# All later conditioning in layer 0 in rows of 1024 columns, three attention scalings on ScalarE, output rows transposed later

## The chip, the cores and the metric

The kernel runs on one core of a Trainium2 chip. The metric is the device time of one execution in microseconds. TensorE (PE) multiplies matrices, with its weight loads shown apart as PEld. VectorE (DVE), ScalarE (ACT) and GpSimd (POOL) work on elements, and SyncE (SP) issues most of the transfers.

## The reference

A two-layer diffusion trunk in fp32 over 640 tokens: 128 of context and 512 latent, 2048 features each. Cut to what matters here:

```
m = silu(cond) @ ada_w[layer] + ada_b[layer]        # one row for context (c_ctx), one for latent (c)
sh, sc, gt = split(m, 3)                            # 3 x 2048 columns
h = rms_norm(x, g) * (1 + sc) + sh
# layer 0: mixer A (windowed attention with a sink logit per head, rotary) and mixer B (gated short convolution)
# layer 1: mixer C (differential attention: o1 - lam * o2, then an RMS norm) and mixer D (dense attention)
p = softmax(q @ k.T * scale)                        # with the sink as one more logit in mixer A
out = concat(branches, each times silu(gate)) @ w_out
x = x + gt * out
```

The input projections have 2048 rows and some fifty tiles of 128 columns in each layer. The results are x of both groups and the new keys and values.

## The kernel before

**Products.** An fp32 operand is split into a rounded high part and a low part. A product is three matmuls into one sum: high weights by high data, high weights by low data, low weights by high data. Tokens stand in columns, in two halves of 320 (`pa`, `pb`).

**Input projection.** `run_tiles` goes over jobs, one for each tile of 128 output columns; layer 0 has 52. A job has four quarters of four 128-row weight blocks. For each quarter `load_raw` fetches 256 KB (SyncE's queue), `split_w` makes `wh` on ScalarE (L232) and `wl` on VectorE (L233), and `proj_q` issues 24 matmuls (L267 to L269), which last some 3.5 us. In layer 0 the first jobs are worked on side by side, and six of them are held as sums in a pool "lead" on the right side of the memory.

**Fill.** Behind each quarter stands a `slot`. It moves the generators on by a step: those that prepare keys, queries and values (`k_gen`, where `kg` is the gained key, multiplied by the rotary tables into `m` at L586 to L590, and transposed on TensorE at L545), the attention that is under way, and a "fill" with a rate, so many steps for each slot.

**Conditioning.** The fill is `ada_on_dve`. It forms blocks of 512 columns of silu(cond) @ ada_w on VectorE: for each of 16 row blocks it loads a tile `adaw` and does a multiply-add into `acc` for each of the two conditions (L202 for the first row block, L204 for the others). Four matmuls with `ones` then add over partitions (L210), ScalarE copies the result, two transposes turn it, and the bias is added. Twelve blocks lie in layer 0 (rate 1.2, a step for each row block). Four lie in layer 1, in halves of 256 columns (rate 0.9, from job 25 on).

**Attention.** `scores` issues the score matmuls `S` (L706 to L710). `soft` takes the negated maximum `nm` on VectorE (L673), scales it (L677 with a sink in layer 0, L675 without in layer 1), takes the exponential on ScalarE (L680, with the row sum `l`), and the reciprocal `rl` (L686). The probabilities `p` are scaled by `rl` in the pair attention (L766, VectorE) and transposed on TensorE (L694) into `T`. Differential attention scales its output by `rls` (L1323, VectorE).

**Output projection.** `project_out` does four tiles of 128 output features singly, and the others in a 2 x 2 form that saves products: `forms` combines halves of the mixed features, and sums of weight blocks (`sx`, `sf`, from L453 on) are multiplied by `run_pairs` (L516 to L518). For a finished tile, `res_load` fetches the old x as `xr`, `res_sum` adds the gated product (L1074), and `finish` in layer 1 transposes the tile with five matmuls `T<-ident,xr` (L545 in `rows_out`), since the results have tokens in rows.

**Order.** The generators set the order in which the program is written, and the language's scheduler moves instructions from there. So the order on an engine is neither the written one nor independent of what else is written.

Of the kernel before, what the change touches and what calls it, by code (L numbers as in the profile page):

```python
# [20 lines left out]
P = 128  # L21
# [24 lines left out]
SPLIT_AHEAD = 3  # L46
N_FILL0 = 12
FILL0 = 1.2
FILL1 = 0.9
FILL1_FROM = 24  # L50


@with_exitstack
def trunk_kernel(ctx: ExitStack, tc: tile.TileContext, I: dict, O: dict):
# [12 lines left out]
    def psT():  # L67
        return pT.tile([P, 512], F32, tag="T", name="T")
# [112 lines left out]

    def ada_on_dve(blocks, tags, parts=1, tie=lambda: None):


        wt, wd = tags[2:5], 512 // parts
        bufs = 3 if wt[0] == wt[1] else 1
        for l, cb in blocks:
            ap = pools["cur"]
            acc = [ap.tile([P, 512], F32, tag=tags[c], name=f"acc{c}", bufs=1) for c in range(2)]
            mark = tie()  # L190
            if mark is not None:
                for c in range(2):
                    V.tensor_copy(acc[c][:, 0:1], mark)
            for i in range(KT * parts):
                kt, h = i % KT, i // KT
                w = ap.tile([P, wd], F32, tag=wt[i % 3], name="adaw", bufs=bufs)
                c0 = cb * 512 + h * wd
                nc.sync.dma_start(w, I["ada_w"][l, kt * P:(kt + 1) * P, c0:c0 + wd])
                for c in range(2):
                    a = acc[c][:, h * wd:(h + 1) * wd]  # L200
                    if kt == 0:
                        V.tensor_scalar(a, w, sT[:, kt, c:c + 1], None, ALU.mult)  # L202
                    else:
                        V.scalar_tensor_tensor(out=a, in0=w, scalar=sT[:, kt, c:c + 1], in1=a,  # L204
                                               op0=ALU.mult, op1=ALU.add)
                yield
            s = psT()
            for g in range(4):
                c, h = g // 2, g % 2
                PE.matmul(s[32 * g:32 * g + 32, 0:256], ones, acc[c][:, h * 256:(h + 1) * 256],  # L210
                          start=True, stop=True, tile_position=(0, 32 * g))
            sb = ap.tile([P, 256], F32, tag=tags[5], name="ada_sb2", bufs=3 if tags[5] == wt[0] else 1)
            A.copy(sb, s[:, 0:256])
            t = psT()
            for j in range(2):
                PE.transpose(t[:, j * P:(j + 1) * P], sb[:, j * P:(j + 1) * P], ident)
            t = t[:, 0:256].rearrange("p (j c h x) -> p h j c x", j=2, c=2, h=2)
            for h in range(2):
                add_bias(l, cb, t[:, h, :, :, 0], h, 2)
            ada_done(l, cb)  # L220
            ready.add((l, cb))
            yield

    ready = set()

    def need(l, n, fill):
        while (l, 8 + n // 4) not in ready:
            next(fill)

# [70 lines left out]
    def run_tiles(jobs, w_ap, make_h, fill=None, rate=0.0, ahead=None, order=(0, 1, 2, 3), before=None,  # L300
                  last=None, by_half=False, trans=[], grace=0, cut=None, summed=None, led=None, fill_from=0, lead_in=None):
        if trans:
# [13 lines left out]
        for ui, (pos, qd, js) in enumerate(units):  # L316
            raws = {n: load_raw(w_ap, jobs[n][0], qd, js) for n in leads[:W_BUFS]}
            if ui == 0 and lead_in:
                lead_in()
            parts = {n: split_w(raws[n]) for n in raws}  # L320
# [350 lines left out]
    def soft(ap, width, s, n, rsc, nsink=None, sink=None):  # L671
        nm = small.tile([P, 1], F32, tag="nm", name="nm")
        V.tensor_reduce(nm, s, axis=AX.X, op=ALU.max, negate=True)  # L673
        if sink is None:
            V.tensor_scalar(nm, nm, rsc, None, ALU.mult)  # L675
        else:
            V.tensor_scalar(nm, nm, rsc, nsink, ALU.mult, ALU.min)  # L677
# [55 lines left out]
    def pair_gen(ap, width, k, banded, emit, done, sinks):  # L733
# [27 lines left out]
        def score(u, j):  # L761
# [3 lines left out]
            p, rl, _ = soft(ap, width, s[:, lo:hi], hi - lo, q[2][u], *sinks[j])  # L765
            V.tensor_scalar(p[:, 0:hi - lo], p[:, 0:hi - lo], rl, None, ALU.mult)  # L766
            ps.setdefault(u, []).append(p)

        for u in range(6):
# [12 lines left out]
            if u < 5:  # L782
# [19 lines left out]

    ada_rest = [(0, cb) for cb in range(8, 12)] + [(1, cb) for cb in (4, 0, 5, 1, 6, 2, 7, 3, 8, 9, 10, 11)]
# [97 lines left out]
    def even_start():  # L901
        close("start")
        open_pool("even")


# [108 lines left out]
    for i in range(4, 8):  # L1014
# [4 lines left out]
    run_tiles(jobs, I["ev_w_in"][0], h0_maker, fill0, FILL0, ada_group, trans=TRANS, grace=GRACE, cut=((0, 2), (2, 4)),  # L1019
              summed=keep, led=even_start)  # L1020
    drain(prep)
    for _ in fill0:
        pass

    N_SINGLE = (4, 4)
# [63 lines left out]
    def project_out(l, maker, finish, last, tail):  # L1089
# [45 lines left out]
        def later(n):  # L1135
            yield
            finish(n)
# [146 lines left out]
    def diff_gen(ap, h, gt):  # L1284
# [28 lines left out]
        def weigh(u):  # L1313
# [62 lines left out]
    for n in range(4):  # L1376
# [14 lines left out]
    def y1_maker(k):  # L1391
        if k == 4:
            for _ in fill1:
                pass
            drain(attn)
# [91 lines left out]
```

## Time and profile before

| | |
|---|---|
| runs, us | 2334.67, 2336.52, 2340.44 (median 2336.52) |
| the profiled execution | 2336.23 us; its span 2334.4 us, 1.8 us lie outside it |
| PE (weight loads) busy | 2286.5 us, 98% (2209.1 us, 95%) |
| DVE busy | 1591.4 us, 68% |
| ACT busy | 950.3 us, 41% |
| POOL busy | 134.4 us, 6% |
| transfers | 321.98 MB, 138 GB/s over the span |

Rows of the profile name the engine, the line, the operation with out<-in, the number of instructions, the busy time and the mean of one in ns, and then the idle time of the engine ahead of them with what ended it. Rows of the timeline have start and length in us, and in brackets the idle time ahead. Rows of the stretches (windows) have the time from start to end in us, the length, the busy time of each engine with its number of instructions, the granted clock of TensorE (1.00 is full), the share of the DMA engines and GB/s.

### The profile page before, as it was taken

How to read it: one execution, taken by the hardware profiler on the slowest of the kernel's cores; microseconds unless marked ns; L12 is line 12 of the kernel's file. 1: busy time of each engine (PE TensorE's matmuls, PEld its weight loads, DVE VectorE, ACT ScalarE, POOL GpSimd, SP SyncE). 2: the span in 40 equal slices, each digit the busy share in tenths (PEclk: the TensorE clock that was granted, in tenths of full speed). 3: DMA queues.
4: the chain of work that ended last, by engine and by line, in shares of the span. 5: the costliest groups of instructions: out<-in, count | busy, mean ns of one | idle time of the engine just before them, and what ended most of it. 6: DMA issues, size and time to landing. Idle time of an engine off the chain costs nothing.

```text
span 2334.4 us, 41910 instructions
## 1 busy us (share of the span) xinstructions
PE 2286.5 (98%) x16092; PEld 2209.1 (95%) x16092; DVE 1591.4 (68%) x3246; ACT 950.3 (41%) x2006; POOL 134.4 (6%) x183
## 2 busy tenths in 40 slices
PE   7999999999999999999999999999999999999999
PEld 5889999999999999899999999999999999999999
DVE  4668887777777774877855755755756754568665
ACT  5335532433422223544554434344334444445443
POOL 1001000000000000000010100101000001000001
PEclk9999999999999999999999999999999999999999
DMA  9986345435355554844431422413323312128542
GB/s 324 292 263 200 105 121 171 142 113 168 118 180 168 169 158 135 263 136 134 150 97 52 144 70 78 141 51 106 112 73 96 102 46 82 49 73 283 156 136 60
DMA packets 399208, 321.98 MB, mean 138 GB/s; under 512 B 18834, under 2 KB 353136, under 8 KB 398496
## 3 DMA queue, kind: packets, MB, share of 16 engines
q1 hardware_dynamic: 391008, 288.94, 41.6%
q0 software_dynamic: 7280, 28.20, 3.2%
q8 instruction: 126, 2.06, 0.4%
q10 hardware_dynamic: 720, 2.16, 0.3%
q14 instruction: 74, 0.61, 0.1%
HBM read 290.79 MB, written 28.44 MB: 137 GB/s over the span
## 4 chain that ended last, share of the span: by engine, by line
PE 48%; DVE 4%; DMA 3%; ACT 1%; issue 1%; POOL 0%; SPq 0%; DVEq 0%; POOLq 0%; ACTq 0%
PE pa L267 4%; PE pb L268 4%; PE pb L267 4%; PE pb L269 4%; PE pa L269 4%; PE pa L268 4%; PE pq L518 4%; PE pq L517 4%; PE pq L516 4%; PE T L694 1%; DMA adaw<-in_ada_w 1%; PE S L706 1%; PE S L708 1%; PE S L707 1%; DMA yin<-yd 1%
## 5 line engine op out<-in xcount | busy, mean ns | idle before, releaser
L232 ACT ACTIVATE wh<-raw 128x512 fp32r<-128x512 f32 (+1 forms) x504 | 303.9, 604 | 782.7 <-PE pb L268 651.8
L267 PE MATMUL pa<-h,wh 128*128 128x320 f32 x1728 | 551.5, 319 | 3.5 <-ACT h L232 3.0
L268 PE MATMUL pa<-h,wh 128*128 128x320 f32 x1728 | 537.4, 311 | 2.8 <-DVE h L233 2.8
L233 DVE TENSOR_TENSOR wl<-raw,wh 128x512 fp32r<-128x512 f32 (+1 forms) x504 | 330.2, 656 | 303.4 <-ACT wh L232 284.0
L269 PE MATMUL pa<-h,wl 128*128 128x320 f32 x1728 | 535.5, 310 | 0.0
L269 PE MATMUL pb<-h,wl 128*128 128x320 f32 x1728 | 535.0, 310 | 0.0
L268 PE MATMUL pb<-h,wh 128*128 128x320 f32 x1728 | 534.9, 310 | 0.0
L267 PE MATMUL pb<-h,wh 128*128 128x320 f32 x1728 | 534.6, 310 | 0.0
L204 DVE SCALAR_TENSOR_TENSOR acc<-adaw,sT,acc 128x512 f32<-128x512 f32 (+1 forms) x600 | 357.4, 641 | 23.0 <-DMA adaw<-in_ada_w 21.8
L267 PEld LDWEIGHTS pa<-h,wh 128*128 128x128 f32 x1728 | 325.4, 188 | 24.6 <-issue 16.6
L268 PEld LDWEIGHTS pa<-h,wh 128*128 128x128 f32 x1728 | 326.1, 189 | 6.3 <-DVE h L233 4.2
L269 PEld LDWEIGHTS pa<-h,wl 128*128 128x128 f32 x1728 | 325.6, 188 | 1.2 <-issue 1.2
L268 PEld LDWEIGHTS pb<-h,wh 128*128 128x128 f32 x1728 | 324.4, 188 | 0.9 <-issue 0.8
L269 PEld LDWEIGHTS pb<-h,wl 128*128 128x128 f32 x1728 | 324.5, 188 | 0.8 <-issue 0.8
L267 PEld LDWEIGHTS pb<-h,wh 128*128 128x128 f32 x1728 | 324.3, 188 | 0.8 <-issue 0.4
L680 ACT ACTIVATE p<-S,nm,rq 128x768 f32<-128x768 f32 (+3 forms) x120 | 101.2, 843 | 108.8 <-DVE nm L675 82.5
L516 PE MATMUL pq<-h,wh 128*128 128x320 f32 x384 | 119.7, 312 | 0.4 <-ACT wh L232 0.4
L518 PE MATMUL pq<-h,wl 128*128 128x320 f32 x384 | 119.2, 310 | 0.7 <-DVE wl L233 0.7
L517 PE MATMUL pq<-h,wh 128*128 128x320 f32 x384 | 119.2, 310 | 0.0
L673 DVE TENSOR_REDUCE nm<-S 128x1 f32<-128x768 f32 (+3 forms) x120 | 92.1, 768 | 21.5 <-PE S L708 20.1
L232 ACT ACTIVATE pth<-T 128x512 fp32r<-128x512 f32 (+1 forms) x132 | 66.0, 533 | 70.5 <-PE T L694 70.5
L516 PE MATMUL pq<-T,wh 128*128 128x320 f32 x288 | 89.5, 311 | 0.1
(307 smaller groups left out, 3483.4 us busy)
## 6 DMA issues: line engine op xcount, KB each, us to landing
raw<-in_od_w_in SPq DMA_DIRECT2D x208, 256.0 KB, 2.9
adaw<-in_ada_w SPq DMA_DIRECT2D x192, 256.0 KB, 3.0
raw<-in_ev_w_in SPq DMA_DIRECT2D x176, 256.0 KB, 3.0
ada<-in_ada_w SPq DMA_DIRECT2D x32, 1024.0 KB, 7.6
adaw<-in_ada_w SPq DMA_DIRECT2D x128, 128.0 KB, 2.4
yd<-y POOLq DMA_DIRECT2D x34, 320.0 KB, 3.0
yin<-yd SPq DMA_DIRECT2D x32, 320.0 KB, 4.7
w<-yd SPq DMA_DIRECT2D x32, 320.0 KB, 4.6
```

What stands on the lines that cost most here:

```text
L204: V.scalar_tensor_tensor(out=a, in0=w, scalar=sT[:, kt, c:c + 1], in1=a, op0=ALU.mult, op1=ALU.add)
L232: A.activation(hi, x, AF.Copy)
L233: V.tensor_sub(lo, x, hi)
L267: PE.matmul(ps, wh[:, i, :], hi[:, sl], start=(j == js[0] if alone else (pos == 0 and j == 0)), stop=False)
L268: PE.matmul(ps, wh[:, i, :], lo[:, sl], start=False, stop=False)
L269: PE.matmul(ps, wl[:, i, :], hi[:, sl], start=False, stop=(j == js[1] - 1 if alone else (pos == 3 and j == 3)))
L516: PE.matmul(ps, wh[:, j, :], hi, start=(new and h == 0 and j == 0), stop=False, **kw)
L517: PE.matmul(ps, wh[:, j, :], lo, start=False, stop=False, **kw)
L518: PE.matmul(ps, wl[:, j, :], hi, start=False, stop=(h == 1 and j == 3), **kw)
L673: V.tensor_reduce(nm, s, axis=AX.X, op=ALU.max, negate=True)
L680: A.activation(p[:, 0:n], s, AF.Exp, scale=rsc, bias=nm, accum_out=l)
L694: PE.transpose(t[:, i * P:(i + 1) * P], p, ident)
```

## The change

**Conditioning.** The sixteen later blocks become eight of 1024 columns, so a row block is one transfer of 512 KB and two VectorE instructions over 1024 columns. All lie in layer 0. Their tiles have a pool of their own, opened when the pool "lead" is closed, behind job 11, and the fill starts there. The fill's step is now one VectorE instruction, not a row block, and its rate is 1.68 for each slot; 34 steps make a block. Layer 1 has no fill.

**Scalings.** `nm` in layer 1, `p` by `rl` in the pair attention and `on` by `rls` are done by ScalarE as an activation with a scale.

**Output rows.** In layer 1 a finished tile waits for two more steps (single tiles) or one more (pairs) ahead of its transposes.

```diff
-N_FILL0 = 12
-FILL0 = 1.2
-FILL1 = 0.9
-FILL1_FROM = 24
+FILL0 = 1.68
...
-            for i in range(KT * parts):
-                kt, h = i % KT, i // KT
-                w = ap.tile([P, wd], F32, tag=wt[i % 3], name="adaw", bufs=bufs)
-                c0 = cb * 512 + h * wd
-                nc.sync.dma_start(w, I["ada_w"][l, kt * P:(kt + 1) * P, c0:c0 + wd])
+            for kt in range(KT):
+                w = ap.tile([P, 1024], F32, tag="adaw", name="adaw", bufs=3)
+                nc.sync.dma_start(w, I["ada_w"][l, kt * P:(kt + 1) * P, cb * 512:cb * 512 + 1024])
                 for c in range(2):
-                    a = acc[c][:, h * wd:(h + 1) * wd]
                     if kt == 0:
-                        V.tensor_scalar(a, w, sT[:, kt, c:c + 1], None, ALU.mult)
+                        V.tensor_scalar(acc[c], w, sT[:, kt, c:c + 1], None, ALU.mult)
                     else:
-                        V.scalar_tensor_tensor(out=a, in0=w, scalar=sT[:, kt, c:c + 1], in1=a,
+                        V.scalar_tensor_tensor(out=acc[c], in0=w, scalar=sT[:, kt, c:c + 1], in1=acc[c],
                                                op0=ALU.mult, op1=ALU.add)
+                    yield
...
-                slot(fill, rate if t > fill_from else 0.0)
+                slot(fill, 0.0 if lp else rate)
...
                 lp.__exit__(None, None, None)
                 lp = None
+                if freed:
+                    freed()
...
-            V.tensor_scalar(nm, nm, rsc, None, ALU.mult)
+            A.activation(nm, nm, AF.Copy, scale=rsc)
...
-            V.tensor_scalar(p[:, 0:hi - lo], p[:, 0:hi - lo], rl, None, ALU.mult)
+            A.activation(p[:, 0:hi - lo], p[:, 0:hi - lo], AF.Copy, scale=rl)
...
-    fill0 = ada_on_dve(ada_rest[:N_FILL0], ("acc0", "acc1", "adaw", "adaw", "adaw", "z"))
-    fill1 = ada_on_dve(ada_rest[N_FILL0:], ("acc0", "acc1", "adaw", "adaw", "adaw", "adaw"), 2,
-                       lambda: mark[-1])
+    fill0 = ada_on_dve([(0, 8), (0, 10), (1, 4), (1, 0), (1, 6), (1, 2), (1, 8), (1, 10)])
...
+    def ada_start():
+        pools["ada_"] = tc.tile_pool(name="ada", bufs=1, side="right")
+        pools["ada"] = pools["ada_"].__enter__()
...
-                yield
+                for _ in range(1 + 2 * l):
+                    yield
                 finish(n)
...
         def later(n):
-            yield
+            for _ in range(1 + l):
+                yield
             finish(n)
...
-            V.tensor_scalar(on, o, rls[u], None, ALU.mult)
+            A.activation(on, o, AF.Copy, scale=rls[u])
...
-    run_tiles(jobs, I["od_w_in"][0], h1_maker, fill1, FILL1, by_half=True, fill_from=FILL1_FROM)
+    run_tiles(jobs, I["od_w_in"][0], h1_maker, by_half=True)
```

VectorE around the first prepared key, before (L572 starts `kg`, L586 is the first product with the rotary tables, L993 to L995 are the convolution's gate, L233 the split of weights, L204 the conditioning):

```order
L572 TENSOR_TENSOR kg<-T,gain_rows 128x512
L575 TENSOR_TENSOR kg<-T,gain_rows 128x128
L577 TENSOR_SCALAR ss<-ss 128x5
L204 SCALAR_TENSOR_TENSOR acc_2347<-adaw,sT,acc_2347 128x512
L579 TENSOR_TENSOR kg<-kg,r 128x640
L233 TENSOR_TENSOR wl<-raw,wh 128x512
L586 TENSOR_TENSOR m_2410<-kg,tables 128x512
L204 SCALAR_TENSOR_TENSOR acc_2348<-adaw,sT,acc_2348 128x512
L993 TENSOR_TENSOR y<-pa,cv 128x320
L994 TENSOR_TENSOR y<-pb,cv 128x192
L995 TENSOR_TENSOR y<-pb,cv 128x128
```

The same place now (the same lines are L553, L556, L558, L560, L567, L975 to L977 and, for the split, L214):

```order
L553 TENSOR_TENSOR kg<-T,gain_rows 128x512
L556 TENSOR_TENSOR kg<-T,gain_rows 128x128
L558 TENSOR_SCALAR ss<-ss 128x5
L560 TENSOR_TENSOR kg<-kg,r 128x640
L567 TENSOR_TENSOR m_2404<-kg,tables 128x512
L214 TENSOR_TENSOR wl<-raw,wh 128x512
L975 TENSOR_TENSOR y<-pa,cv 128x320
L536 SCALAR_TENSOR_TENSOR y<-gt_t,sum_425 128x320 x2
L976 TENSOR_TENSOR y<-pb,cv 128x192
L977 TENSOR_TENSOR y<-pb,cv 128x128
```

The two conditioning rows are gone from this place, since the fill has not started there, and one product row (L536) has come in.

VectorE in a softmax of layer 0, from one score's maximum (L673) to the next score's, before (L677 scales `nm`, L684 adds the sink's share to the sum, L686 is the reciprocal, L766 scales `p`):

```order
L673 TENSOR_REDUCE nm<-S 128x1
L204 SCALAR_TENSOR_TENSOR acc_5560<-adaw,sT,acc_5560 128x512
L677 TENSOR_SCALAR nm<-nm,rq_5530,nsink 128x1
L204 SCALAR_TENSOR_TENSOR acc_5559<-adaw,sT,acc_5559 128x512
L204 SCALAR_TENSOR_TENSOR acc_5560<-adaw,sT,acc_5560 128x512
L684 TENSOR_TENSOR l<-l,es 128x1
L204 SCALAR_TENSOR_TENSOR acc_5559<-adaw,sT,acc_5559 128x512
L686 RECIPROCAL rl<-l 128x1
L233 TENSOR_TENSOR wl<-raw,wh 128x512
L766 TENSOR_SCALAR p<-p,rl 128x512
L673 TENSOR_REDUCE nm<-S 128x1
```

The same place now (L654, L658, L665 and L667 are those lines; L191 is the conditioning):

```order
L654 TENSOR_REDUCE nm<-S 128x1
L214 TENSOR_TENSOR wl<-raw,wh 128x512
L658 TENSOR_SCALAR nm<-nm,rq_5418,nsink 128x1
L191 SCALAR_TENSOR_TENSOR acc_5253<-adaw,sT,acc_5253 128x1024
L665 TENSOR_TENSOR l<-l,es 128x1
L191 SCALAR_TENSOR_TENSOR acc_5254<-adaw,sT,acc_5254 128x1024
L667 RECIPROCAL rl<-l 128x1
L214 TENSOR_TENSOR wl<-raw,wh 128x512
L654 TENSOR_REDUCE nm<-S 128x1
```

Four adds of 512 columns have become two of 1024, the split of weights stands inside the chain in place of an add, and the scaling of `p` has left VectorE.

TensorE where the single output tiles of layer 1 end, around the fourth group of five transposes `T<-ident,xr`, before (L516 to L518 multiply the paired form):

```order
L516 MATMUL pq<-h_24503,wh 128x320
L517 MATMUL pq<-h_24503,wh 128x320
L518 MATMUL pq<-h_24503,wl 128x320
L545 MATMUL T<-ident,xr 128x128 x5
L516 MATMUL pq<-h_24712,wh 128x320
L517 MATMUL pq<-h_24712,wh 128x320
```

The same group now (L526; L497 to L499 are the paired form):

```order
L497 MATMUL pq<-h_23715,wh 128x320
L498 MATMUL pq<-h_23715,wh 128x320
L499 MATMUL pq<-h_23715,wl 128x320
L526 MATMUL T<-ident,xr 128x128 x5
L497 MATMUL pq<-h_23924,wh 128x320
L498 MATMUL pq<-h_23924,wh 128x320
```

Its neighbours look alike, but 36 matmuls of the paired form stand between it and what was there before them, where 12 did: by TensorE's rows the first four groups stood at 13572, 13585, 13598 and 13683, and stand now at 13601, 13638, 13675 and 13712.

More of the change, by code (lines that the diff above doesn't have):

```diff
@@ L180, in ada_on_pe, with ada_on_dve @@
         ada_done(l, cb, h, n)
-    def ada_on_dve(blocks, tags, parts=1, tie=lambda: None):
-        wt, wd = tags[2:5], 512 // parts
-        bufs = 3 if wt[0] == wt[1] else 1
+    def ada_on_dve(blocks):
         for l, cb in blocks:
[L188 to L191, printed above, removed]
-                for c in range(2):
-                    V.tensor_copy(acc[c][:, 0:1], mark)
-            for i in range(KT * parts):
-                kt, h = i % KT, i // KT
-                w = ap.tile([P, wd], F32, tag=wt[i % 3], name="adaw", bufs=bufs)
-                c0 = cb * 512 + h * wd
-                nc.sync.dma_start(w, I["ada_w"][l, kt * P:(kt + 1) * P, c0:c0 + wd])
-                for c in range(2):
-                    a = acc[c][:, h * wd:(h + 1) * wd]
+            ap = pools["ada"]
+            acc = [ap.tile([P, 1024], F32, tag=f"acc{c}", name=f"acc{c}", bufs=1) for c in range(2)]
+            for kt in range(KT):
+                w = ap.tile([P, 1024], F32, tag="adaw", name="adaw", bufs=3)
+                nc.sync.dma_start(w, I["ada_w"][l, kt * P:(kt + 1) * P, cb * 512:cb * 512 + 1024])
+                for c in range(2):
@@ L207, in ada_on_dve @@
[L207 to L221, printed above, removed]
-            yield
[L224 to L228, printed above, removed]
+                    yield
+            for b in range(2):
+                s = psT()
+                for g in range(4):
+                    c, h = g // 2, g % 2
+                    PE.matmul(s[32 * g:32 * g + 32, 0:256], ones, acc[c][:, b * 512 + h * 256:b * 512 + (h + 1) * 256],
+                              start=True, stop=True, tile_position=(0, 32 * g))
+                sb = ap.tile([P, 256], F32, tag="sb", name="ada_sb2", bufs=1)
+                A.copy(sb, s[:, 0:256])
+                t = psT()
+                for j in range(2):
+                    PE.transpose(t[:, j * P:(j + 1) * P], sb[:, j * P:(j + 1) * P], ident)
+                t = t[:, 0:256].rearrange("p (j c h x) -> p h j c x", j=2, c=2, h=2)
+                for h in range(2):
+                    add_bias(l, cb + b, t[:, h, :, :, 0], h, 2)
+                ada_done(l, cb + b)
+                yield
@@ L300, in run_tiles @@
     def run_tiles(jobs, w_ap, make_h, fill=None, rate=0.0, ahead=None, order=(0, 1, 2, 3), before=None,
-                  last=None, by_half=False, trans=[], grace=0, cut=None, summed=None, led=None, fill_from=0, lead_in=None):
+                  last=None, by_half=False, trans=[], grace=0, cut=None, summed=None, led=None, freed=None):
         if trans:
@@ L317, in run_tiles @@
             raws = {n: load_raw(w_ap, jobs[n][0], qd, js) for n in leads[:W_BUFS]}
-            if ui == 0 and lead_in:
-                lead_in()
             parts = {n: split_w(raws[n]) for n in raws}
@@ L1019, in trunk_kernel @@
     run_tiles(jobs, I["ev_w_in"][0], h0_maker, fill0, FILL0, ada_group, trans=TRANS, grace=GRACE, cut=((0, 2), (2, 4)),
-              summed=keep, led=even_start)
+              summed=keep, led=even_start, freed=ada_start)
     drain(prep)
@@ L1023, in trunk_kernel @@
         pass
+    close("ada_")
     N_SINGLE = (4, 4)
@@ L1392, in y1_maker @@
         if k == 4:
-            for _ in fill1:
-                pass
             drain(attn)
```

2 lines of the change are left out of this document (removed).

## The prediction

> **What bounds the kernel now.** I read the page's busy times first, then a table by stretches, then the waits of TensorE, then the timeline at those waits.
>
> ```profile
> PE 2286.5 (98%) x16092; PEld 2209.1 (95%) x16092; DVE 1591.4 (68%) x3246; ACT 950.3 (41%) x2006; POOL 134.4 (6%) x183
> ```
> ```profile
> 186.00:272.00 86.00, 83.91 (x585) 78.91 (x584) 74.47 (x164) 49.04 (x119) 8.19 (x7) 0.98 0.45 131
> 272.00:913.00 641.00, 639.74 (x4504) 626.27 (x4503) 469.03 (x914) 203.07 (x427) 18.33 (x22) 1.00 0.49 147
> ...
> 1245.00:2100.00 855.00, 847.72 (x5930) 827.38 (x5929) 529.27 (x1179) 364.79 (x808) 59.03 (x73) 1.00 0.29 85
> 2100.00:2175.00 75.00, 67.61 (x454) 65.72 (x453) 58.75 (x104) 35.72 (x60) 5.49 (x9) 0.99 0.85 270
> ```
>
> The columns are PE, PEld, DVE, ACT and POOL, then the clock, the DMA share and GB/s. TensorE sets the time: it is idle for 2334.4 − 2286.5 = 47.9 us of the span. The change leaves its matmuls as they are (the same number on TensorE by the order), so it can win only idle time and slow clock. In layer 0's steady stretch (272 to 913 us) the idle time is 641.0 − 639.74 = 1.3 us, in layer 1's (1245 to 2100) 7.3 us, and in the first part of the last projection (2100 to 2175) 7.4 us. TensorE's waits say which operands come late, first in layer 0's stretch (its only row), then in layer 1's:
>
> ```profile
> PE T L545 <- DVE m L590: 1.1, 1, 1.1
> ```
> ```profile
> PE T L545 <- DVE m L590: 3.0, 3, 1.9
> PE S L706 <- ACT p L680: 1.0, 1, 1.0
> PE T L545 <- DVE k1l L233: 0.9, 1, 0.9
> ```
>
> The columns are the total in us, the number of waits, and the longest. The conditioning stands in VectorE's queue around these operands; the waits outside the two stretches are shown below at their places.
>
> **The conditioning, its volume.** VectorE's groups, each shape apart:
>
> ```profile
> L204 DVE SCALAR_TENSOR_TENSOR acc<-adaw,sT,acc 128x512 f32<-128x512 f32 x360 | 254.8, 748 | 12.8 <-DMA adaw<-in_ada_w 12.2
> L204 DVE SCALAR_TENSOR_TENSOR acc<-adaw,sT,acc 128x256 f32<-128x256 f32 x240 | 102.6, 481 | 10.2 <-DMA adaw<-in_ada_w 9.5
> ```
>
> 256 more columns cost 748 − 481 = 267 ns, so an add of 1024 should take 748 + 2 × 267 = 1282 ns, an estimate. Before, the adds cost 254.8 + 102.6 = 357 us; now 8 × 15 × 2 = 240 of them cost 308 us. That is 49 us less on VectorE, but all of it in layer 0. Layer 0 held 360 of the 600 adds, 254.8 us; with at most 308 in its place in the steady stretch VectorE is busy for some (469 + 53) / 641 = 81% there, against 73% before, and it still has room. Its transfers become half as many of twice the size on SyncE's queue, and four blocks more lie in the layer, 16 MB over some 700 us: 24 GB/s on top of 147, at a DMA share of 0.49, which I cost at nothing. The last few steps are drained behind the last job, two or three adds on VectorE, where TensorE still has that job's matmuls. With 1.3 us of idle time in that stretch, nothing is to be won there but the wait of 1.1 us at a key; it can only be lost.
>
> **The conditioning, its place.** At the first key, TensorE and VectorE:
>
> ```profile
> 206.18 0.66 PE L545 MATMUL T<-ident,m 128*128 128x128 f32 x4 [1.99 <-DVE m L590]
> ...
> 207.45 0.47 PE L267 MATMUL pa<-h,wh 128*128 128x320 f32 x1
> ...
> 209.31 0.47 PE L268 MATMUL pa<-h,wh 128*128 128x320 f32 x1
> ```
> ```profile
> 202.31 0.75 DVE L204 SCALAR_TENSOR_TENSOR acc<-adaw,sT,acc 128x512 f32<-128x512 f32 x1
> ...
> 205.44 0.69 DVE L590 TENSOR_TENSOR m<-m,m 128x512 f32<-128x512 f32 x1
> ```
>
> Such an add of 0.75 us stands twice inside the key's chain (both are in the rows of the order), more stand ahead of it, and TensorE waits 1.99 us for `m`. In the new order neither stands here, since the fill has not begun; one product row of about half a microsecond has come in. The chain should end some 1.0 to 1.5 us earlier. Behind the wait, seven matmuls take 209.31 − 207.45 = 1.86 us, 0.27 each, where the usual spacing is about half of that (0.14 between the two TensorE rows of the softmax below), so the clock was slow for some 3 us, which cost about 1.2. I take 1.2 of wait and 1.2 of clock: −2.4, bounds 0 (another operand is as late) and −3.2. The key at 407 us has its wait of 1.1: the transposes stand ten rows of TensorE later now, 1.5 us of matmuls, so −1.1, bounds 0 and −1.1.
>
> In layer 1 no conditioning is left. One row shows what it did there:
>
> ```profile
> 1662.76 2.46 DVE L204 SCALAR_TENSOR_TENSOR acc<-adaw,sT,acc 128x256 f32<-128x256 f32 x6 [1.15 <-DMA adaw<-in_ada_w]
> ```
>
> Six adds in one piece, behind a transfer, put the score's maximum back, and the wait of 1.0 us for the exponential to free `S` follows from it. Of the waits shown there (3.0 + 1.0 + 0.9 = 4.9) I take half, −2.5: most of a key's chain is its own work, with adds of 0.48 us between, against a wait of up to 1.9, so the other half should come back. Bounds 0 and −4.9.
>
> **The scalings.** On VectorE they go away; on ScalarE a scaling has no row yet, so I bound it by neighbours:
>
> ```profile
> L766 DVE TENSOR_SCALAR p<-p,rl 128x512 f32<-128x512 f32 x16 | 7.8, 485 | 0.1
> ```
> ```profile
> L232 ACT ACTIVATE wh<-raw 128x512 fp32r<-128x512 f32 x440 | 277.7, 631 | 726.4 <-PE pb L268 612.9 <-issue 46.9 <-PE pq L517 29.7
> ...
> L680 ACT ACTIVATE p<-S,nm,rq 128x512 f32<-128x512 f32 x16 | 12.5, 780 | 13.4 <-DVE nm L677 11.4 <-PE T L694 2.0
> L683 ACT ACTIVATE es<-sink,nm 128x1 f32<-128x1 f32 x40 | 11.6, 289 | 0.0
> ```
>
> `p` over 512 columns lies between the plain copy (0.63) and the exponential with its two operands and row sum (0.78), against 0.49 on VectorE; I take 0.78, so +0.30 in a chain. `nm` should take the 0.29 of `es`, of the same one column. The 180 new activations, none above 1.0 us, bring ScalarE to 950 + at most 100 us, 45%: it does not become the bound, and ScalarE is idle for over half of layer 1's stretch (364.79 busy of 855). The scaling of `p` adds a wait to its queue, for `rl`. Behind it stand splits `wh` of weights that TensorE needs a quarter or more later, and the copies of the transposed `p`, which need the scaling anyway. So I cost the scalings at nothing in layer 1 (bounds −1 and +2); what hides them is that TensorE has projection matmuls between scores and transposes. The Trainium skill, "ScalarE: Activation LUTs", section Rules for kernel authors, speaks against this edit: multiplications belong on VectorE, not on ScalarE. The rows agree on the time of one instruction; they do not say that this instruction is waited for.
>
> **The softmax of layer 0**, where wide adds and the slower scaling meet. A pair's second score, VectorE, and the transposes that wait for it:
>
> ```profile
> 455.82 0.70 DVE L673 TENSOR_REDUCE nm<-S 128x1 f32<-128x512 f32 x1
> 456.42 0.76 DVE L204 SCALAR_TENSOR_TENSOR acc<-adaw,sT,acc 128x512 f32<-128x512 f32 x1
> ...
> 459.99 0.50 DVE L766 TENSOR_SCALAR p<-p,rl 128x512 f32<-128x512 f32 x1
> ```
> ```profile
> 460.55 0.31 PE L267 MATMUL pa<-h,wh 128*128 128x320 f32 x1
> 460.69 0.82 PE L694 MATMUL T<-ident,p 128*128 128x128 f32 x6
> ```
>
> From the maximum to the scaled `p` it takes 460.49 − 455.82 = 4.67 us, and the transposes start 0.20 us behind that, without a wait. By the order, four adds of 0.76 less an overlap of 0.1, 2.6 in all, lay in this chain; now two of 1.28 do, with that overlap 2.4, the split of 0.6 stays, and `p` is 0.30 longer: about the same length. The first score's chain loses the scaling on VectorE, so the second begins up to 0.5 earlier. I take +0.5 over the layer for places where the pieces fall badly (bounds −2 and +14, which is a third of a microsecond at each of 40 scores, the count of `es` above).
>
> **The output rows.**
>
> ```profile
> 2154.55 0.77 PE L545 MATMUL T<-ident,xr 128*128 128x128 f32 x5 [2.10 <-ACT ot L1409]
> ...
> 2173.83 0.90 PE L545 MATMUL T<-ident,xr 128*128 128x128 f32 x3 [3.36 <-DVE xr L1074]
> ...
> 2177.29 0.31 PE L516 MATMUL pq<-h,wh 128*128 128x320 f32 x1
> ```
> ```profile
> 2171.01 1.29 DVE L453 TENSOR_TENSOR sx<-w,raw 128x512 f32<-128x512 f32 x2 [3.87 <-issue]
> ...
> 2173.94 1.28 DVE L233 TENSOR_TENSOR wl<-sx,wh 128x512 fp32r<-128x512 f32 x2
> ```
>
> Both waits, 2.10 and 3.36, are at transposes that now stand later, the fourth group behind 24 more matmuls. But 12 of these use `sx`, which VectorE forms at 2171.0, behind a wait for loaded weights (marked issue) that the change does not touch. They can start when `wl` is split, by the new order right behind the sums, at about 2173.4, where they started at 2177.29. Of these 3.9 us one group of transposes (0.77) is only put off, and a wait of about 3.5 us now stands ahead of `sx`, with a slow clock of about 1 us behind it: −2.2. Bounds −1 and, if the load comes earlier too, −2.1 − 3.4 − 1.2 = −6.7.
>
> **The sum:** −2.4 − 1.1 − 2.5 + 0 + 0.5 − 2.2 = −7.7 against the profiled run's 2336.2 (its span 2334.4 and 1.8 outside), which stands 0.3 us below the median of 2336.5. The forecast is 2336.4 − 7.7, 2328.7 us. Its own range is 2325 to 2333.
>
> **The rivals.**
>
> *Slower: the softmax of layer 0 becomes what TensorE waits for.* The margin at 460.49 is 0.20 us. If VectorE meets an add of 1.28 at two places where one of 0.75 lay (2 × 0.53 = 1.06), and the scaling adds 0.30, a pair's second score is 1.36 − 0.20 = 1.16 us late. At 20 pairs that is 23 us: 2328.7 + 23, about 2352; where only half of the pairs are late, 2340. It decides from 0.20 us of lengthening on. For it: VectorE's load in layer 0 rises, and the new order has the adds between maximum, sum and reciprocal. Against it: the sum of the chain above, and the stretch's 1.3 us of idle time, which says that most places had more room. The Trainium skill, "Perfetto Trace Analysis", section Optimizing Scalar/DVE Operations, gives the rule behind it: where VectorE is not saturated but makes other engines wait, instructions should be broken up, and this change joins them. Chance 0.20.
>
> *The waits come back where they were.* The keys wait for their chain, and the output for the loaded weights; then only the 407 us wait and a little of the others goes: 2334 to 2337. For it: most of a key's chain is its own work, and `sx` waits for the load. Chance 0.16.
>
> *More room than TensorE's idle time tells.* The weight loads are idle for 2334.4 − 2209.1 = 125 us, 27.6 of it in layer 1's stretch. If half of those 27.6 are small hitches that VectorE's adds cause, 14 us go in place of layer 1's 2.5: 2317, and with a third of them 2322; I take 2321. Against it: layer 0's stretch has fewer of them (14.7 of 641) with more adds. Chance 0.14.
>
> **How the numbers follow.** The forecast has 0.50, the rivals 0.20, 0.16 and 0.14. The bound of 0.3% is about what a measurement of this kernel can tell from no change, 7.0 us: 2329.5 and 2343.5. Of the forecast's 0.50 about 0.28 lies below 2329.5; with the third rival faster is 0.42. Slower has 0.20, of which some lies below 2343.5 but the bad ends of the other cases make up for it; the rest, 0.38, is the same. The range leaves out the heavier half of the slow rival and the tail of the third: 2319 to 2343.
>
> **What would show it.** Right: no wait for `m` at 206 us and the granted clock of 186 to 272 at 1.00; layer 1's idle time at 5 us or less; the waits at 2154 and 2174 gone, one for `sx` in their place. Wrong: rows of waits for `p` on ScalarE or VectorE in layer 0, or adds that take clearly over 1.3 us; no change of the idle time in layer 1; a wait at the conditioning's matmuls when its last rows are drained behind layer 0.

## The result and the profile after

| | before | after |
|---|---|---|
| median, us | 2337.2 | 2318.6 |
| ratio of the runs | | 0.9919 (0.9901 to 0.9937) |
| measured again | 2335.6 | 2318.6, ratio 0.9933 (0.9921 to 0.9946) |
| PE busy of the span | 2286.5 of 2334.4 | 2282.3 of 2319.2 |

The kernel became faster by 16 to 19 us. The direction was the forecast's; the size is twice the forecast's 7.8 or more, and 2318.6 lies just below the range.

The busy times of the profile after:

```profile
PE 2282.3 (98%) x16092; PEld 2209.7 (95%) x16092; DVE 1484.3 (64%) x2674; ACT 1035.5 (45%) x2186; POOL 131.4 (6%) x183
```

The same stretches as before (PE, PEld, DVE, ACT, POOL, clock, DMA share, GB/s):

```profile
186.00:272.00 86.00, 82.14 (x579) 77.27 (x579) 67.34 (x135) 51.87 (x116) 6.17 (x7) 1.00 0.49 153
272.00:913.00 641.00, 639.88 (x4514) 623.58 (x4516) 509.70 (x788) 227.90 (x474) 20.56 (x23) 1.00 0.56 171
1245.00:2100.00 855.00, 854.41 (x5975) 838.63 (x5975) 399.62 (x777) 429.15 (x955) 56.42 (x73) 1.00 0.23 68
2100.00:2175.00 75.00, 75.00 (x514) 74.24 (x513) 64.60 (x110) 38.92 (x67) 6.77 (x11) 1.00 0.90 284
```

TensorE's idle time in layer 1's stretch fell from 7.3 us to 0.6, and in the start of the last projection from 7.4 to 0. Layer 0's stretch has 1.1 for 1.3, with VectorE busy for 80% (the estimate was 81%). Only from 186 to 272 us, where the fill now starts beside the first softmax, it rose, from 2.1 to 3.9 us (3.1 in a second profile). One add of 1024 columns took 1.28 us, as estimated:

```profile
L191 DVE SCALAR_TENSOR_TENSOR acc<-adaw,sT,acc 128x1024 f32<-128x1024 f32 x240 | 300.0, 1278 | 0.0
```

What TensorE still waits for, over the whole span (first rows):

```profile
PE T L120 <- DMA rows_a<-in_ada_b: 7.6, 1, 7.6
PE T L121 <- DMA rows_b<-in_d_q_norm: 4.6, 1, 4.6
PE pa L248 <- DVE sum L315: 3.8, 2, 2.5
PE T L526 <- DVE m L571: 2.6, 4, 1.0
PE pa L248 <- ACT h L213: 2.0, 3, 0.9
PE T L1199 <- POOL r L1195: 1.8, 2, 1.4
PE S L687 <- ACT p L661: 1.6, 1, 1.6
```

No row for `xr` or `ot` of the single tiles is left, and `m` costs 2.6 us for 6.9. One row is new and belongs to the change: the wait for `p` at `S`, 1.6 us at 242 us.

Both kernels issue the same number of matmuls in almost the same order, so the start of the n-th can be compared. From the trace, in us against the first profile of before:

| profile | up to 200 us | layer 0, to 915 | to 1293 | layer 1, to 2088 | last projection, to 2243 | rest |
|---|---|---|---|---|---|---|
| after | +5.4 | −2.8 | −0.5 | −6.6 | −10.0 | −0.7 |
| after, second profile | +2.0 | −2.8 | +0.5 | −6.7 | −9.8 | −0.8 |
| before, second profile | +0.3 | 0.0 | −1.0 | −0.9 | −2.5 | +0.1 |
| before, third profile | +2.9 | −1.6 | +1.9 | +1.8 | −2.1 | 0.0 |

The two lower rows are the same kernel as the reference: they show what one execution differs from another by, up to 3 us in a stretch. The first profile of before was dear in the last projection by some 2.3 us. What is left to the change is about 7 us in layer 1 and 7 to 8 in the last projection. In layer 0 it is 1 to 3, no more than the same kernel differs by.

The last projection's part is more than waits. There the three profiles of before lose 7.3, 5.1 and 5.4 us to waits of TensorE, and in each of them its granted clock falls to 0.50 for some 3.4 us (at 2174 to 2176 us in the first, 2153 to 2155 in the second, 2178 to 2180 in the third), which costs some 1.7 us more, an estimate: half of that time. The two profiles of after have neither.

### The profile page after: what moved, and what is told of

Same layout as the page of the kernel before. It is cut to its first block, busy times and chain, and to the rows that moved or that the text cites. A ratio compares the mean times of both kernels' runs of the same rounds, so it can differ in the third digit from the quotient of the medians.

```text
span 2319.2 us, 41035 instructions
## 1 busy us (share of the span) xinstructions
PE 2282.3 (98%) x16092; PEld 2209.7 (95%) x16092; DVE 1484.3 (64%) x2674; ACT 1035.5 (45%) x2186; POOL 131.4 (6%) x183
## 4 chain that ended last, share of the span: by engine, by line
PE 91%; DVE 3%; DMA 2%; ACT 2%; issue 1%; POOL 1%; SPq 0%; DVEq 0%; POOLq 0%; ACTq 0%
PE pa L248 11%; PE pb L248 10%; PE pb L249 10%; PE pa L249 10%; PE pb L250 10%; PE pa L250 10%; PE pq L499 4%; PE pq L498 4%; PE pq L497 4%; PE T L675 2%; PE S L687 1%; PE S L689 1%; PE S L688 1%; PE T L166 1%; PE T L526 1%; PE T L736 1%
## 5 line engine op out<-in xcount | busy, mean ns | idle before, releaser
L214 DVE TENSOR_TENSOR wl<-raw,wh 128x512 fp32r<-128x512 f32 (+1 forms) x504 | 329.8, 655 | 388.5 <-ACT wh L213 356.2
L191 DVE SCALAR_TENSOR_TENSOR acc<-adaw,sT,acc 128x1024 f32<-128x1024 f32 x240 | 300.0, 1278 | 0.0
L497 PE MATMUL pq<-h,wh 128*128 128x320 f32 x384 | 120.4, 314 | 1.0 <-ACT wh L213 1.0
L499 PE MATMUL pq<-h,wl 128*128 128x320 f32 x384 | 119.6, 311 | 0.8 <-DVE wl L214 0.8
L654 DVE TENSOR_REDUCE nm<-S 128x1 f32<-128x768 f32 (+3 forms) x120 | 91.9, 766 | 24.9 <-PE S L689 24.1
```

What stands on the lines that cost most here:

```text
L191: V.scalar_tensor_tensor(out=acc[c], in0=w, scalar=sT[:, kt, c:c + 1], in1=acc[c], op0=ALU.mult, op1=ALU.add)
L214: V.tensor_sub(lo, x, hi)
L497: PE.matmul(ps, wh[:, j, :], hi, start=(new and h == 0 and j == 0), stop=False, **kw)
L499: PE.matmul(ps, wl[:, j, :], hi, start=False, stop=(h == 1 and j == 3), **kw)
```

## The experiments

**One part at a time.** Four kernels: before with the late rows alone (the lines of the diff in `job` and `later`), with the three scalings alone, with the conditioning alone, and the changed kernel without the late rows.

> The kernel before with one part of the change: the output rows of layer 1 transposed later. Theory A (the parts act each at its own place, and the late rows give nearly all of what the last projection gained): the waits of 2.1 and 3.4 us at T<-ident,xr go and no wait for sx takes their place; 8 to 10 us less, 2328 us, all of it behind 2085 us of the span. Theory B (the term of the prediction: the loads for sx keep their time, and the wait comes back there): 2 us less, 2335 us, with a new wait of 3 us at the paired matmuls. Theory C (the last projection gained because TensorE's other operands came earlier through the rest of the change): 0 to 2 us less, and the wait at h of about 1.5 us at 2140 us stays.

> The kernel before with one part of the change: the three scalings of attention on ScalarE. Theory A (they are beside other work): within 2 us of before, layer 1's idle time of 7 us stays. Theory D (layer 1's gain of 6.6 us comes from VectorE being freed of 50 us of scalings there): 4 to 7 us less, in 1245 to 2100 us. The prediction's slower rival: 10 us more or worse, with waits for p in layer 0.

> The kernel before with one part of the change: the conditioning (all later blocks in layer 0, 1024 columns, own pool, a step for each instruction). Theory A: layer 1's waits for m, S and k1l go, 6 to 7 us less there, layer 0 within 2 us; 2330 us, and the waits at T<-ident,xr of 2.1 and 3.4 us stay. Theory D (the scalings did it): 2 to 3 us less.

> The changed kernel with the output rows transposed as early as before. Theory A: the last projection is as before (waits of 2 and 3.4 us at T<-ident,xr), the rest as changed: 2327 to 2328 us. Theory C (the last projection gains through the rest): 2319 to 2321 us, waits at T<-ident,xr under 1 us.

| kernel | median, us | ratio to before (interval) | us less, from the ratio |
|---|---|---|---|
| late rows alone | 2331.5 | 0.9985 (0.9975 to 0.9994) | 3.5 |
| scalings alone | 2331.4 | 0.9983 (0.9973 to 0.9992) | 4.0 |
| conditioning alone | 2327.9 | 0.9969 (0.9957 to 0.9981) | 7.2 |
| all but the late rows | 2324.1 | 0.9953 (0.9938 to 0.9968) | 11.0 |

The parts add up within their intervals: 3.5 + 4.0 + 7.2 = 14.7, against 15.6 to 18.9 for the whole. With the conditioning alone, one row is left in 1245 to 2085 us:

```profile
PE S L687 <- ACT p L661: 0.3, 1, 0.3
```

With the late rows alone, the last projection (2085 to 2200 us) keeps one wait worth naming, at the paired matmuls:

```profile
PE pq L516 <- DVE xr L1074: 1.6, 1, 1.6
```

Theory A, that each part acts at its own place, holds for the conditioning: by the start of the n-th matmul, layer 1 took 5.1 us less with it alone. The six profiles of kernels that have the scalings too show 6.6 to 6.9, so some 1.5 us of the 6.7 come with the scalings. For the late rows it holds as to the two waits, but in the median they give less than half of the 8 to 10 us that it expected. No phase of slow clock lies in the last projection with them alone. The conditioning has a wait of its own at 242 us, of 2.0 to 2.1 us for `p`, in both kernels that have it here; the scalings alone have none there.

**Place or width.** Before, with all blocks in layer 0 and narrow, as the edit of two constants:

```diff
-N_FILL0 = 12
-FILL0 = 1.2
+N_FILL0 = 16
+FILL0 = 1.6
```

> The kernel before with all sixteen later blocks in layer 0, as before in 512 columns and a step for each row block (16 blocks at rate 1.6); neither the scalings nor the late rows. It tells place from width. Theory A (what layer 1 gains is the absence of conditioning there): layer 1's waits go as in the conditioning alone, 5 us less in 1245 to 2100 us; layer 0 then takes 16 x 31 x 0.74 = 367 us of adds and VectorE is busy for some 90% there, so some of it may be lost in layer 0: 2329 to 2333 us. Rival (the width, with fewer and longer instructions, brings the gain): 2334 us or more, since layer 0 loses what layer 1 wins.

2329.0 us, ratio 0.9972 (0.9958 to 0.9985), 6.5 us less. No wait is left in 1245 to 2085 us, and VectorE's load in layer 0 rises, to 85% where some 90% was expected:

```profile
272.00:913.00 641.00, 639.23 (x4511) 623.13 (x4510) 544.00 (x1056) 204.75 (x439) 19.95 (x23) 1.00 0.58 170
1245.00:2100.00 855.00, 854.00 (x5966) 836.64 (x5965) 440.69 (x916) 370.82 (x818) 57.60 (x75) 1.00 0.23 68
```

TensorE is idle in layer 0's stretch for 1.8 us, against 1.3 before. Layer 1 took 5.3 us less by the start of the n-th matmul, as with wide adds. So the gain is the place; the width adds nothing that can be told (6.5 against 7.2).

**The step.** The changed kernel with one step for each row block, so two wide adds for each step:

```diff
-FILL0 = 1.68
+FILL0 = 0.89
...
                 for c in range(2):
...
-                    yield
+                yield
```

> The changed kernel with a fill step for each row block (two adds of 1024 columns in one piece, 2.5 us) in place of one for each add, at a rate of 0.89 for 1.68. If the fine step is needed to keep the adds out of the way of layer 0's softmax and keys, as the prediction's slower rival would have it: waits for p, m or S in layer 0 and 5 to 20 us more. If the order is the scheduler's anyway: within 2 us of the changed kernel.

2318.2 us, ratio 0.9926 (0.9903 to 0.9948): the same as the changed kernel. But the edit hardly reached the engine: up to 915 us VectorE has the conditioning in 114 single instructions, 41 pieces of two and 20 of three, against 107, 43 and 21 in the changed kernel. The fine step is not needed, since it is not what sets the order; what longer pieces would cost is not told.

**The fill later.** The changed kernel with the fill held until job 14:

```diff
-FILL0 = 1.68
+FILL0 = 1.8
+FILL_FROM = 25
...
-                slot(fill, 0.0 if lp else rate)
+                slot(fill, 0.0 if lp or t < FILL_FROM else rate)
```

> The changed kernel with the fill held until job 14 of layer 0 (rate 1.8 for 1.68), so that no conditioning lies beside the first pair of attention. If the wait of 1.6 to 2.1 us for p at 242 us (seen in each kernel with the conditioning all in layer 0) comes from the first adds beside the first softmax, it goes, 1 to 2 us less than the changed kernel, 2316.5 to 2317.5 us; if it comes from the scaling of p on ScalarE, it stays. VectorE's load is higher behind it: new waits in layer 0 would cost it again.

2320.2 us, ratio 0.9939 (0.9925 to 0.9953), not distinct from the changed kernel. The edit didn't do what it was for: in its trace the adds still stand beside the first softmax, and the wait is 1.4 us.

```profile
236.71 2.47 DVE L192 SCALAR_TENSOR_TENSOR acc<-adaw,sT,acc 128x1024 f32<-128x1024 f32 x2
```

The scheduler puts them there, not the slot: the first adds stand where they stood, 4.7 us earlier like the work around them. What causes this wait stays argued. It is there with the conditioning alone (2.0 us) and in the changed kernel with `p` back on VectorE (2.0 us), so it is not the scaling of `p`. With narrow adds all in layer 0 it is 0.4 us, which points at the wide adds.

**The queue of the last projection.** Before, with `xr` of layer 1 loaded through GpSimd's queue:

```diff
-        nc.sync.dma_start(st["xr", n], xdram[n] if l else ...
+        (nc.gpsimd if l else nc.sync).dma_start(st["xr", n], xdram[n] if l else ...
```

> The kernel before with one edit of its own: the old x (xr) of layer 1 is loaded through GpSimd's queue, not SyncE's. The rows of TensorE stay as before. Theory E (in SyncE's queue a load of xr that waits for a buffer stood ahead of the weights for sx, and that delay, not the weights' own transfer, was the 3.4 us at T<-ident,xr): the weights of the paired form are issued 4 us or so earlier, the wait of 3.4 us goes or falls under 1 us, the one of 2.1 us stays; 3 to 5 us less. The prediction's step (the load of these weights keeps its time): no change.

2336.0 us, ratio 1.000 (0.9991 to 1.001); the waits are 3.1 and 3.0 us. The weights for `sx` were issued at 2162.60 us, no sooner than before, and used at 2170.35. Theory E fell: the place in SyncE's queue was not the delay. What was? In the timeline of before, SyncE's issues (start, and the length to the end of the last of the row):

```profile
2158.29 3.76 SPq L1069 DMA_DIRECT2D xr<-xd  x1
2162.96 3.15 SPq L429 DMA_DIRECT2D w<-in_od_w_out  x2
```

`sx` started at 2171.0, 8.0 us behind the issue of its weights at 2162.96 (6.8 and 6.7 us in the other two profiles of before). In this time the DMA engines were fully busy (share 1.04 in 2160 to 2165 us). Among the loads there are the stores of the first output rows, issued by GpSimd; the larger one of each tile:

```profile
2154.79 0.77 POOL L1411 DMA_DIRECT2D out_y_sample<-ot  x1 [44.62 <-ACT ot L1410]
2157.40 0.76 POOL L1411 DMA_DIRECT2D out_y_sample<-ot  x1 [1.31 <-ACT ot L1410]
2160.24 0.76 POOL L1411 DMA_DIRECT2D out_y_sample<-ot  x1 [1.56 <-ACT ot L1410]
```

**Without those stores.** Before, leaving out the stores of the first four output tiles:

```diff
+        if n > 3:
             nc.gpsimd.dma_start(O["y_sample"][0, :, n * P:(n + 1) * P]...
             nc.gpsimd.dma_start(O["y_prompt"][0, :, n * P:(n + 1) * P], ot[:, 4, :])
```

> The kernel before without the stores of the first four output rows of layer 1 (their transposes and copies stay; these rows of the result are left out). In the kernel before the weights A21 for sx were issued at 2162.96 us and used at 2171.0, 8 us later; with the late rows it took 5 us. Theory H (the stores of the rows stand in the way of this transfer, with the DMA engines fully busy there): sx 2 to 3 us earlier, the wait of 3.4 us at T<-ident,xr falls to about 1, 2 to 4 us less. Theory I (the transfer is not what held sx; the forms on VectorE and ScalarE, which the rows' copies and sums delay, were): the wait of 3.4 us stays, within 1 us of before.

2331.8 us, ratio 0.9986 (0.9975 to 0.9997), 3.3 us less. SyncE's issue and VectorE's use:

```profile
2160.68 3.00 SPq L429 DMA_DIRECT2D w<-in_od_w_out  x2
```
```profile
2164.72 1.29 DVE L453 TENSOR_TENSOR sx<-w,raw 128x512 f32<-128x512 f32 x2 [0.23 <-DVE wl L233]
```

4.0 us from issue to use, not 6.7 to 8.0, and no wait at `xr` is left; the one of 1.9 for `ot` stays. The share of the DMA engines from 2155 to 2165 us fell from 0.97 to 0.79. Theory H holds: the stores of the early rows shared the DMA engines with the weights that TensorE needed next. With the late rows alone the same way took 5.0 us, and in the changed kernel 4.2, from 2155.93 to 2160.12 us. There the stores come one tile at a time, with more matmuls between them; one of the larger ones is issued beside the transfer, the next behind it:

```profile
2157.04 0.76 POOL L1394 DMA_DIRECT2D out_y_sample<-ot  x1 [5.96 <-ACT ot L1393]
2162.93 0.76 POOL L1394 DMA_DIRECT2D out_y_sample<-ot  x1 [4.60 <-ACT ot L1393]
```

**Single tiles or pairs.** Before, with late rows for the four single tiles only.

> The kernel before with late rows for the four single tiles alone; the pairs' rows as early as before. Theory A in detail (the gain lies at the first four groups of transposes, where both waits were): as the late rows in full, 7 us less behind 2085 us. Rival (the pairs' rows, which are many more, give part of it): 2 us or more less gain than the late rows in full.

2329.0 us, ratio 0.9976 (0.9965 to 0.9987), 5.6 us less: all of the late rows' gain, as far as it can be told. The pairs' part shows no gain of its own.

**Which scaling.** Before with `p` alone, `nm` alone and `on` alone, and the changed kernel with `p` back on VectorE.

> The kernel before with one of the three scalings on ScalarE: p by the reciprocal, in the pair attention. The three together gave 4 us, 2.4 of them behind 2085 us, where the last pairs of attention end. Theory F (it is p: 40 scalings of VectorE less in layer 1, and the splits of h behind them come earlier): 2 to 4 us less, the wait at h of 1.5 us at 2140 us is gone. Theory G (nm or the output of differential attention did it): within 1 us of before.

> The kernel before with one scaling on ScalarE: nm in layer 1 (80 instructions of one column). Theory J (nm gives it: the maximum's scaling no longer queues on VectorE behind other work, so the exponential starts earlier): 3 to 4 us less, some of it as a shorter wait for the exponential at S or at y in layer 1. Theory K (the output of differential attention gives it): within 1.5 us of before.

> The kernel before with one scaling on ScalarE: the output of differential attention by rls (20 instructions of 256 columns). Theory K: 3 to 4 us less. Theory J: within 1.5 us of before. If neither of the two kernels gains, the 4 us of the three together lie in the order of the last projection, which the scheduler makes anew for each kernel, and not in a scaling.

> The changed kernel with p scaled on VectorE again; nm and the output of differential attention stay on ScalarE. If p on ScalarE costs, as it seemed on the kernel before (1.1 us more): 1 to 3 us less than the changed kernel, 2316 us. If it helps VectorE in the full layer 0, where VectorE is busy for 80%: 1 to 4 us more, with waits in layer 0. If it is beside other work: within 1 us of 2318.6.

| kernel | median, us | ratio to before (interval) |
|---|---|---|
| `p` alone | 2337.2 | 1.0005 (0.9993 to 1.0016) |
| `nm` alone | 2330.8 | 0.9981 (0.9972 to 0.9991) |
| `on` alone | 2335.6 | 1.0004 (0.9995 to 1.0014) |
| after, `p` on VectorE | 2319.2 | 0.9925 (0.9911 to 0.9938) |

`nm` gives all of it, 4.4 us; the other two give nothing that can be told, and `p` costs nothing. The rows of `nm` and `p` on ScalarE, in the changed kernel:

```profile
L656 ACT ACTIVATE nm<-nm,rq 128x1 f32<-128x1 f32 x80 | 23.5, 294 | 59.1 <-DVE nm L654 59.1
L747 ACT ACTIVATE p<-p,rl 128x512 f32<-128x512 f32 x16 | 11.6, 725 | 8.3 <-DVE rl L667 8.2
```

With `nm` alone the exponential of layer 1 starts 0.52 us behind the end of the maximum, on average from 1245 to 2100 us, against 0.57 to 0.58 in the three profiles of before. Where TensorE gains by that is not seen. Its wait at `S` is 0.3 us, but 1.0, none and 1.0 in the profiles of before, and none with `on` alone. By the start of the n-th matmul, layer 1 took 1.9 us less and the last projection 4.5; with `on` alone, which gains nothing, it is 1.2 and 4.2. So how `nm` makes the kernel faster stays open.

**The same kernels again.** The changed kernel and the kernel before, for further profiles.

> The changed kernel again, for a second profile. Its first profile lost 3.6 us at 151 us of the span, where a job's first weights came late, ahead of anything that the change moves on TensorE. If that is chance, it is not there again, and the span of the profile is some 3 us shorter at the same waits elsewhere (none in layer 1's stretch, none behind 2085 us); if the change causes it, it comes again.

> The kernel before, unchanged, for a second profile. If the waits that the prediction's terms rest on are fixed by the order: 2.0 us for m at 206 us, 3.0 + 1.0 + 0.9 in layer 1, 3.4 and 2.1 at T<-ident,xr, each within 0.5. If some are chance (transfers that land earlier or later): those at 206 us and in the last projection differ by 1 to 4 us, those of layer 1, where the DMA engines are 29% busy, do not.

> The kernel before, unchanged, for a third profile; expected as in the second.

The 3.6 us at 151 us in the first profile of after did not come again (1.1 in the second, by the same comparison). Of before's waits in layer 1, two come each time, for `m` 3.0, 2.9 and 3.3 and for `k1l` 0.9 three times; that for `S` is 1.0, none and 1.0. In the last projection the wait for `xr` was 3.4, 1.6 and 2.9, that for `ot` 2.1, 2.2 and 2.1, that for `h` 1.8, 1.3 and 0.4.

## Why the prediction was right or wrong

**What bounds the kernel: right.** The change won idle time of TensorE, 11 us of the 15 by which the profiled span is shorter, and its matmuls are as many as before. The other 4 us are busy time of the same matmuls and stay unexplained.

**The volume in layer 0: right.** The estimated add of 1282 ns took 1278, and VectorE's 81% was 80%. Layer 0 as a whole lost nothing.

**The first key: the size right, in part by luck.** −2.4 was forecast, half of it wait and half slow clock. In both profiles of after the stretch from 200 to 218 us took 2.3 less than in the first of before. But the wait for `m` fell only from 2.0 to 1.0, where none was to be left. And the slow clock comes in two of the three profiles of before alone: the granted clock from 208 to 210 us is 0.50, 0.50 and, behind a wait as long, 1.00. A forecast made from the third profile would have had no such term. 1.3 us came back at 242 us, at the wait for `p`; the term for the softmax had +0.5.

**The key at 407 us: mis-sized,** −1.1 for about −0.3. Its transposes stand later, and so does what they wait for, 0.85 us for 1.1:

```profile
412.04 0.66 PE L526 MATMUL T<-ident,m 128*128 128x128 f32 x4 [0.85 <-DVE m L571]
```

**Layer 1: mis-sized, −2.5 for some −6.7,** 5 of it from the conditioning. The step that failed is "so the other half should come back": with the conditioning alone, 0.3 us of wait is left there. The conditioning of before stands in layer 1 from 1294 to 1838 us (from the 25th quarter on, not the 25th job). All of TensorE's waits in layer 1 lie in that stretch, 6.3 us with the three smaller rows beside the 4.9, and so does the gain. I counted the adds inside a key's chain and not those ahead of it. VectorE at the key of 1332 us, before:

```profile
1330.99 1.28 DVE L204 SCALAR_TENSOR_TENSOR acc<-adaw,sT,acc 128x256 f32<-128x256 f32 x3 [1.04 <-DMA adaw<-in_ada_w]
1332.19 0.69 DVE L572 TENSOR_TENSOR kg<-T,gain_rows 128x512 f32<-128x512 f32 x1
```

and the same key after:

```profile
1336.95 0.69 DVE L553 TENSOR_TENSOR kg<-T,gain_rows 128x512 f32<-128x512 f32 x1 [0.83 <-ACT junk L551]
```

TensorE's transposes that feed it start at 1328.49 before and 1334.71 after. The chain began 3.7 us behind them, at the end of three adds that had waited for their transfer, and now 2.2 us behind them: 1.5 us that no count of adds inside the chain shows. The wait of 1.9 is that and one add of 0.48 inside the chain. The rival that more goes than TensorE's waits tell (0.14) was nearest to the result, 2321, but for another reason than it gave: the weight loads' idle time in that stretch fell from 27.6 us to 16.4, 11.2, of which TensorE's own idle time is 6.7. The Trainium skill, "Perfetto Trace Analysis", section Identifying the Most-Contended Engine, holds busy matmuls for a poor measure of how much room there is, and weight loads for a better one. In this stretch 6.7 us went, near TensorE's own 7.3 of idle time, and 16.4 us of the weight loads' idle time are still there.

**The output rows: mis-sized, −2.2 for 3.5 alone and 4.6 or more on top of the other parts** (11.0 against 15.6). The step that failed is the wait for loaded weights "that the change does not touch". It does: the stores of the rows that it puts off shared the DMA engines with this load, and without them it took 4.0 us, not 6.7 to 8.0. Where I put a wait of 3.5 us, ahead of the products with `sx`, TensorE waited 1.6 us with the late rows alone and not at all in the changed kernel, and the slow clock that I put behind it did not come in either.

**The scalings: wrong, 0 for 4.0,** and 3.8 on top of the conditioning (11.0 against 7.2). The step that failed is "I cost the scalings at nothing in layer 1". The bounds (−1 and +2) were taken from busy engines and from `p`. The edit that counts is the smallest, `nm`, one column. Its wait ahead of the exponential was in the page before, with 82.5 us of ScalarE's idle time behind `nm`, and I did not follow it:

```profile
L680 ACT ACTIVATE p<-S,nm,rq 128x768 f32<-128x768 f32 (+3 forms) x120 | 101.2, 843 | 108.8 <-DVE nm L675 82.5
```

That `p` costs 0.72 us on ScalarE (between the bounds of 0.63 and 0.78) and that this is hidden was right. The rule of the Trainium skill, "ScalarE: Activation LUTs", section Rules for kernel authors, against multiplications on ScalarE holds for the time of one instruction (0.72 against 0.49) and did not decide.

**The slower rival: did not come.** One wait of 1.6 us for `p` came in layer 0, not twenty of 1.2. At 85% of VectorE, with narrow adds, TensorE's idle time in layer 0's stretch was 1.8 us.

**The range.** Its lower end left out the case in which two terms are at their far bounds together; layer 1 and the output rows both were, and the scalings were beyond theirs.

## What to carry to other kernels

Filler work on a side engine costs where it stands ahead of a chain that the main engine waits for, so count what is queued before the chain's first instruction, not only what is inside it. When transfers are full, ask of each store that the order puts early which load it shares the engines with: what looks like a slow load can be cured by moving a store. Read a wait in a DMA-bound stretch from several profiles before it becomes a term of a sum; here the same kernel's wait was 1.6, 2.9 and 3.4 us, and the slow clock behind a wait came or stayed away. Where a scheduler makes the order, read the order of each experiment ahead of its time: two edits here were meant to move the adds and hardly did.

## What the runs showed of the hardware

A load of 512 KB took 8.0, 6.8 and 6.7 us from issue to use beside row stores, in three profiles, and 4.0 us without them, with the same number of loads around it. TensorE's granted clock fell to 0.50 for some 3.4 us in the last projection in each profile of before, and in neither of after, where no wait was left there. Moving 80 scalings of one column from VectorE (0.21 us each) to ScalarE (0.29 us each, longer by themselves) made the kernel 4.4 us faster; that the value no longer waits behind other work in VectorE's queue is a possible reason, not a shown one.
